# A gated hybrid encoder block on one core: the output product by seven products of quarters, and the first head's group four groups later

## Chip, core and metric

One Trainium2 chip, of which the kernel uses one core. The metric is the time of one execution in microseconds (us). A core has a matrix engine (TensorE, PE in the profile, PEld for its weight loads), a vector engine (VectorE, DVE), a scalar engine (ScalarE, ACT), GpSimd (POOL) and SyncE (SP), which here only issues transfers. Each engine works through its own row of instructions in order and waits at semaphores for the others; DMA engines move data between DRAM and the on-chip memory.

## What is computed

For 512 tokens of width 2048, all in float32:

```python
n = rmsnorm(x, norm_w)
proj = n @ w_in                       # gated DeltaNet, mLSTM and gate columns
y_a = gdn_branch(...)                 # 8 heads, conv of width 5, delta rule in chunks of 64, both directions
y_b = mlstm_branch(...)               # 8 heads, both directions
gates = sigmoid(gates + gate_bias)
merged = gates[0] * (y_a @ w_branch_gdn) + gates[1] * (y_b @ w_branch_mlstm)
x = x + merged @ w_out                # merged 512 x 2048, w_out 2048 x 2048
return rmsnorm(x, final_norm_w)
```

The change is in `merged @ w_out` and in where one head of `gdn_branch` is placed.

## The kernel before

Every large product is done with operands split in two: a high part, rounded to TensorE's fast float32 format, and a low part, the rest. A product of two split operands is three matmuls, high x high, high x low and low x high. Weights come in blocks of 512 KB (128 x 1024 numbers). `Block.load` (L160) brings a block into one of four raw buffers (`wr`), four blocks ahead (`LOAD_AHEAD`). `Block.split`, two blocks ahead (`SPLIT_AHEAD`), casts it to `wh` on ScalarE (L175) and subtracts to `wl` on VectorE (L176); three buffers each. Then the block's matmuls read both, first all of `wh`, then all of `wl`. A list `blocks` holds the blocks in the order of use: input projection, gates, branch products, output product.

Beside this stream run the heads, written as a generator (`master`). `tick()` lets it go on by one step after every fourth matmul of the projections (`TICK`), so the program order mixes head work and projection matmuls; a scheduler of the framework then sets each engine's row by its own priorities. `gdn_pre(h)` (the group at L485 to L498: products `pgm`, transposes `px`, `pq` of one GDN head) waits four ticks after `gv` of its head is done. `conv` (L427) makes `cv` by four tap operations on VectorE (L431) and an activation on ScalarE (L445). `ml_head(h)` (L802) does one mLSTM head: it loads `e` from `d_row`, makes `kw` (L853), states `msp` (L867) copied to `cn` (L872), and the outputs `ph`.

`br_evac` (L1007) multiplies the branch products by the gates and, for the second branch, splits their sum `merged` into `mh` and `ml`.

The output product has four column blocks e of 512, each with eight weight blocks of two k-tiles. Per block and row tile t of four there are six matmuls (`o_mms`, L1054), four row tiles accumulate in four PSUM banks, and after the eighth block `residual` (L1060) adds the product to x on VectorE, squares it on ScalarE and multiplies by the norm's weights. For e = 3 the eight blocks are kept, so that each row tile runs its 48 matmuls in one go and is then finished (`finish`: L1068 to L1076) while the next one runs. The tail of the kernel is the finish of row tile 3.

## Time and profile before

| | us |
|---|---|
| median of 3 runs | 1692.74 (1691.44 to 1692.97) |
| the profiled execution | 1691.47 |
| its span, first to last instruction | 1689.7 |
| TensorE busy | 1663.9 |
| VectorE busy | 863.7 |
| ScalarE busy | 627.2 |
| first matmul of the output product, from the span's start | 1506.07 |
| DMA traffic | 251.93 MB, mean 149 GB/s |

The span is what lies between the first and the last instruction; the execution's own time is 1.8 us longer. TensorE is the engine that is nearly always busy, the others are far from it on the mean, but they need not be in every stage. Matmuls overlap, so the duration of one (0.39 us) is longer than the step from one to the next. "Granted clock" is the share of full speed that TensorE's clock was given.

### The profile page before, as it was taken

How to read it: one execution, taken by the hardware profiler on the slowest of the kernel's cores; microseconds unless marked ns; L12 is line 12 of the kernel's file. 1: busy time of each engine (PE TensorE's matmuls, PEld its weight loads, DVE VectorE, ACT ScalarE, POOL GpSimd, SP SyncE). 2: the span in 40 equal slices, each digit the busy share in tenths (PEclk: the TensorE clock that was granted, in tenths of full speed). 3: DMA queues.
4: the chain of work that ended last, by engine and by line, in shares of the span. 5: the costliest groups of instructions: out<-in, count | busy, mean ns of one | idle time of the engine just before them, and what ended most of it. 6: DMA issues, size and time to landing. Idle time of an engine off the chain costs nothing.

```text
span 1689.7 us, 20934 instructions
## 1 busy us (share of the span) xinstructions
PE 1663.9 (98%) x8218; PEld 1397.3 (83%) x8218; DVE 863.7 (51%) x1259; ACT 627.2 (37%) x973; POOL 84.0 (5%) x117
## 2 busy tenths in 40 slices
PE   6999999999999999999999999999999999999998
PEld 6878888888888888888888888888888888888886
DVE  6866555669993344322444544544544444443342
ACT  6654444423333223334343344334234322222231
POOL 1110111000100000001000000000000000000000
PEclk9999999999999999999999999999999999999999
DMA  7576767594548767335343334434335544453322
GB/s 191 148 203 190 206 173 193 141 302 139 137 131 214 211 217 225 102 92 177 96 114 107 107 102 116 118 92 116 87 101 160 184 149 147 139 193 144 100 100 100
DMA packets 334204, 251.93 MB, mean 149 GB/s; under 512 B 38968, under 2 KB 294329, under 8 KB 333081
## 3 DMA queue, kind: packets, MB, share of 16 engines
q1 hardware_dynamic: 327952, 238.39, 49.4%
q10 hardware_dynamic: 6153, 12.19, 2.2%
q8 instruction: 65, 1.06, 0.3%
q14 instruction: 34, 0.28, 0.1%
HBM read 207.32 MB, written 43.16 MB: 148 GB/s over the span
## 4 chain that ended last, share of the span: by engine, by line
PE 94%; DMA 2%; issue 1%; DVE 1%; ACT 1%; SPq 0%; ACTq 0%; POOL 0%; POOLq 0%; DVEq 0%
PE pj_m L212 26%; PE pj_mg L212 19%; PE pj_br L212 10%; PE wo L1054 9%; PE pj_gq L212 5%; PE pj_gz L212 5%; PE pj_gv L212 5%; PE pj_gk L212 4%; PE og L685 1%; PE vps L708 1%; PE ph L887 1%; DMA wr<-in_w_in_dram 1%; PE pgm L491 1%; PE pj_gk L1175 1%; PE ph L886 1%
## 5 line engine op out<-in xcount | busy, mean ns | idle before, releaser
L176 DVE TENSOR_TENSOR wl<-wr,wh 128x1024 fp32r<-128x1024 f32 x270 | 331.3, 1228 | 461.9 <-ACT wh L175 175.9
L175 ACT CAST wh<-wr 128x1024 fp32r<-128x1024 f32 x270 | 284.1, 1053 | 682.7 <-PE pj_m L212 207.5
L212 PE MATMUL pj_m<-nth,wh 128*128 128x512 f32 x640 | 250.5, 391 | 0.0
L212 PE MATMUL pj_m<-ntl,wh 128*128 128x512 f32 x640 | 249.1, 389 | 0.0
L212 PE MATMUL pj_mg<-nth,wh 128*128 128x512 f32 x512 | 204.0, 399 | 0.0
L212 PE MATMUL pj_mg<-ntl,wh 128*128 128x512 f32 x512 | 199.8, 390 | 0.0
L212 PE MATMUL pj_m<-nth,wl 128*128 128x512 f32 x640 | 160.2, 390 | 0.0
L212 PEld LDWEIGHTS pj_m<-nth,wh 128*128 128x128 f32 x640 | 120.2, 188 | 24.5
L212 PEld LDWEIGHTS pj_m<-ntl,wh 128*128 128x128 f32 x640 | 120.2, 188 | 24.4
L212 PEld LDWEIGHTS pj_m<-nth,wl 128*128 128x128 f32 x640 | 119.6, 188 | 24.6
L212 PE MATMUL pj_mg<-nth,wl 128*128 128x512 f32 x512 | 126.7, 389 | 0.0
L212 PEld LDWEIGHTS pj_mg<-nth,wl 128*128 128x128 f32 x512 | 96.1, 188 | 20.3
L212 PEld LDWEIGHTS pj_mg<-nth,wh 128*128 128x128 f32 x512 | 96.3, 188 | 18.9
L212 PEld LDWEIGHTS pj_mg<-ntl,wh 128*128 128x128 f32 x512 | 96.3, 188 | 18.4
L1054 PE MATMUL wo<-wh,mh 128*128 128x512 f32 x256 | 100.0, 391 | 0.0
L1054 PE MATMUL wo<-wh,ml 128*128 128x512 f32 x256 | 99.6, 389 | 0.0
L212 PE MATMUL pj_br<-yh,wh 128*128 128x512 f32 x256 | 99.6, 389 | 0.0
L212 PE MATMUL pj_br<-yl,wh 128*128 128x512 f32 x256 | 99.6, 389 | 0.0
L1054 PE MATMUL wo<-wl,mh 128*128 128x512 f32 x256 | 72.9, 390 | 0.2 <-DVE wl L176 0.2
L1019 DVE TENSOR_TENSOR mgr<-pj_br,mgr 128x512 f32<-128x512 f32 x32 | 22.1, 692 | 86.5 <-PE pj_br L212 86.5
L212 PE MATMUL pj_br<-yh,wl 128*128 128x512 f32 x256 | 63.2, 389 | 0.0
L1054 PEld LDWEIGHTS wo<-wl,mh 128*128 128x128 f32 x256 | 48.0, 188 | 10.9 <-DVE wl L176 0.6
(321 smaller groups left out, 2513.6 us busy)
## 6 DMA issues: line engine op xcount, KB each, us to landing
wr<-in_w_in_dram SPq DMA_DIRECT2D x206, 512.0 KB, 4.1
wr<-in_w_out_dram SPq DMA_DIRECT2D x32, 512.0 KB, 3.7
hr<-d_head SPq DMA_DIRECT2D x16, 768.0 KB, 5.8
d_gate<-gt ACTq DMA_DIRECT2D x32, 256.0 KB, 2.2
e<-d_row SPq DMA_DIRECT2D x8, 1024.0 KB, 5.5
mgr<-d_gate SPq DMA_DIRECT2D x32, 256.0 KB, 4.8
wr<-in_w_branch_gdn_dram SPq DMA_DIRECT2D x16, 512.0 KB, 4.4
wr<-in_w_branch_mlstm_dram SPq DMA_DIRECT2D x16, 512.0 KB, 4.5
```

The lines of the kernel that those rows point to most:

```text
L175: nc.scalar.copy(hi[:, 0:m], self.raw[:, 0:m])
L176: nc.vector.tensor_tensor(lo[:, 0:m], self.raw[:, 0:m], hi[:, 0:m].bitcast(F32), op=ALU.subtract)
L212: nc.tensor.matmul(ps[0:m, :], l, r, start=(first and n == 0), stop=(last and n == len(jobs) - 1))
L491: nc.tensor.matmul(pgm[t // 2][:, t % 2], ckq[:, 0, cs], ckq[:, :, cs], start=True, stop=True)
L685: nc.tensor.matmul(po[:, t], l, r, start=not opened, stop=last)
L708: nc.tensor.matmul(vps[:, d], xt[:, d, t], rhs[d], start=True, stop=True)
L886: nc.tensor.matmul(ph[:, j - q0, :], e4[:, d, 1, t, :], cn[d][1][:, n - 1, :], start=True, stop=False)
L887: nc.tensor.matmul(ph[:, j - q0, :], e4[:, d, 0, t, :], vv[:, t, :], start=(n == 0), stop=True)
L1019: nc.vector.tensor_tensor(g_, ps, g_, op=ALU.mult)
L1054: nc.tensor.matmul(ps, l[:, kt, ts_], r, start=(kt == 0 and l is mh and r is hv), stop=(kt == NK - 1 and r is lv))
L1175: nc.tensor.matmul(pk[:, ts_], w, act[:, kt, ts_], start=not opened, stop=last)
```

## The change

**The output product.** `merged` (512 x 2048) and `w_out` (2048 x 2048) are cut into quarters: token halves (256 rows) by even and odd 128-wide k-tiles on one side, even and odd k-tiles by column halves within each half e of 1024 columns on the other. By the scheme of Strassen in Winograd's form the 2 x 2 product of quarters is made with seven products in place of eight; four of the seven use sums of quarters of `w_out`, four use sums of quarters of `merged`. Each of the two halves e is done so, in the order of products `OUT_ORDER`. A product is four weight blocks of two row tiles p, 12 matmuls per block. The number of weight blocks goes from 32 to 56.

**Sums of w_out.** They depend on nothing but the input, and are made in sixteen parts within `ml_head`, two per head: `quarter_load` (three transfers on SyncE, 1 MB in all), `quarter_sums` (three VectorE operations), `quarter_store` (one transfer of 1 MB on SyncE into a DRAM buffer `d_t`). The blocks of the last stage are then loaded from `w_out` or `d_t`.

**Sums of merged.** `br_evac` keeps `merged` in float32 (`mf`), casts what the first products need and adds the quarters in place; `s_split` splits the four sums during the first eight blocks of the last stage. x and the final norm's weights come in during the first half, in parts.

**Evacuation.** Products are added to x as they come (`out_evac`, `add_to`), products 1, 6 and 7 by way of a running sum `u`. Row tiles 0 and 1 are done with product 3 of the second half; the last product keeps its four blocks and runs row tile by row tile, so that only tiles 2 and 3 are finished at the end.

**The first head's group.** `gdn_pre(0)` waits for eight ticks, not four.

```diff
@@ gdn_pre
-        for _ in range(4):
+        for _ in range(8 if h == 0 else 4):
             yield
@@ ahead of ml_head
+    def quarter_load(q):
+        e, j = q // 8, q % 8
+        qt = st["p3"][1].tile([P, 4, 512], F32, tag="qt", name=f"qt{q}", bufs=2)
+        c = e * 1024
+        nc.sync.dma_start(qt[:, 0:2].rearrange("p a c -> p (a c)"), wo4[j, 0][:, c:c + 1024])
+        nc.sync.dma_start(qt[:, 2], wo4[j, 1][:, c + 512:c + 1024])
+        nc.sync.dma_start(qt[:, 3], wo4[j, 1][:, c:c + 512])
+    def quarter_sums(q):
+        ts = st["p3"][1].tile([P, 4, 512], F32, tag="qs", name=f"qs{q}", bufs=2)
+        nc.vector.tensor_tensor(ts[:, 0:2], qt[:, 1:3], qt[:, 0:2], op=ALU.subtract)
+        nc.vector.tensor_tensor(ts[:, 2], qt[:, 2], ts[:, 0], op=ALU.subtract)
+        nc.vector.tensor_tensor(ts[:, 3], ts[:, 2], qt[:, 3], op=ALU.subtract)
+    def quarter_store(q):
+        nc.sync.dma_start(d_t[q // 8, :, q % 8].rearrange("i p c -> p i c"), st.pop(("qs", q)))
@@ ml_head
+        quarter_load(2 * h)
         while f"m0{h}" not in done:
             yield
         e = p3.tile([P, 2, 2, T], F32, tag="e", name=f"e{h}", bufs=2)
...
+        quarter_load(2 * h + 1)
         for _ in range(6):
             yield
+        quarter_sums(2 * h)
...
+        quarter_store(2 * h)
         while f"m1{h}" not in done:
             yield
+        quarter_sums(2 * h + 1)
...
+        quarter_store(2 * h + 1)
@@ br_evac, second branch
+                nc.vector.tensor_tensor(mf[:, n], st["g", 0], g_, op=ALU.add)
+                (hi, lo), src = (st["a2"], mf[:, n]) if n % 2 else (st["a1"], mf[:, n, 0:256])
+                nc.scalar.copy(hi[:, j], src)
+                nc.vector.tensor_tensor(lo[:, j], src, hi[:, j].bitcast(F32), op=ALU.subtract)
+                if n % 2:
+                    nc.vector.tensor_tensor(a22, a21, a22, op=ALU.add)
+                    nc.vector.tensor_tensor(a21, a11, a21, op=ALU.subtract)
+                    nc.vector.tensor_tensor(a11, a22, a11, op=ALU.subtract)
+                    nc.vector.tensor_tensor(a12, a12, a11, op=ALU.subtract)
@@ output product
+    OUT_ORDER = ((1, 4, 2, 5, 6, 3, 7), (1, 5, 2, 6, 3, 7, 4))
+    def s_split(n):
+        nc.scalar.copy(hi[:, js], src)
+        nc.vector.tensor_tensor(lo[:, js], src, hi[:, js].bitcast(F32), op=ALU.subtract)
+    def out_mms(i, p, jobs, first, last):
+        for n, (j, v, lo) in enumerate(jobs):
+            for a in (ah,) if lo else (ah, al):
+                nc.tensor.matmul(st["po", i, p], a[:, j, ts_], v, ...)
+            if (e, i) == (1, 4):
+                st["last"] = st.get("last", []) + his + los
+                if b < 3:
+                    return
+                for p in range(2):
+                    out_mms(i, p, st["last"], True, True)
+                    out_evac(e, i, p)
+                return
+            for jobs in (his, los):
+                for p in range(2):
+                    out_mms(i, p, jobs, b == 0 and jobs is his, b == 3 and jobs is los)
+    for e in range(2):
+        for pos in range(7):
+            for b in range(4):
+                blocks.append(Block(... out_src(e, OUT_ORDER[e][pos], b) ..., 2, 512, out_use(e, pos, b), ...))
@@ finish
-        nc.scalar.activation(rt[:, 0:768], rt[:, 0:768], AF.Identity, scale=fr)
-        nc.scalar.dma_start(rows[:, 0:768], rt[:, 0:768])
+        nc.scalar.activation(rt[0][t], rt[0][t], AF.Identity, scale=fr)
+        nc.scalar.dma_start(rows[:, 0:1024], rt[0][t])
```

How the rows of the engines move, at three places. The numbers behind the names count tiles and differ between the two kernels.

TensorE at the first GDN head's group, before: the transposes of `cv` (`px`) stand behind 16 matmuls on `wh` and one on `wl` of the unit `gk`, after that the unit `gq` begins.

```order
L212 MATMUL pj_gk_861<-ntl,wh_819 128x512
L212 MATMUL pj_gk_861<-nth,wl_820 128x512
L495 MATMUL px_889<-ident,cv_847 128x128 [waits Activation_49]
L495 MATMUL px_889<-ident,cv_847 128x128 x3
L212 MATMUL pj_gk_861<-nth,wl_820 128x512 x7
L212 MATMUL pj_gq_991<-nth,wh_857 128x512 [waits DVE_49]
L212 MATMUL pj_gq_991<-ntl,wh_857 128x512
L212 MATMUL pj_gq_991<-nth,wh_857 128x512
```

The same place after:

```order
L500 MATMUL px_911<-ident,ckq_691 128x128 x4
L503 MATMUL pq_921<-ident,ckq_691 128x128 x4
L217 MATMUL pj_gk_862<-nth,wh_820 128x512
L217 MATMUL pj_gk_862<-ntl,wh_820 128x512
L500 MATMUL px_912<-ident,cv_848 128x128 [waits Activation_49]
L500 MATMUL px_912<-ident,cv_848 128x128 x3
L217 MATMUL pj_gk_862<-nth,wh_820 128x512
L217 MATMUL pj_gk_862<-ntl,wh_820 128x512
L217 MATMUL pj_gk_862<-nth,wl_821 128x512 x8
L217 MATMUL pj_gq_976<-nth,wh_858 128x512 [waits DVE_49]
L217 MATMUL pj_gq_976<-ntl,wh_858 128x512
```

The group stands later in the unit: ten matmuls of `gk` are left behind `px`, where there were seven.

VectorE in the same group, before, between the taps of `cv` (L431) and the `la` products, and then after, where L436 and L510 are those lines:

```order
L431 SCALAR_TENSOR_TENSOR ca_g_848<-pj_gv_789,cwg,ca_g_848 128x510 [waits Activation_49]
L505 TENSOR_TENSOR la_903<-pgm_882,dec_589 128x512 [waits PE_49,Pool_49]
L431 SCALAR_TENSOR_TENSOR ca_g_848<-pj_gv_789,cwg,ca_g_848 128x511 [waits DVE_49]
L505 TENSOR_TENSOR la_903<-pgm_882,dec_589 128x512 [waits Pool_49]
L431 SCALAR_TENSOR_TENSOR ca_g_848<-pj_gv_789,cwg,ca_g_848 128x511 [waits DVE_49]
L505 TENSOR_TENSOR la_903<-pgm_883,dec_589 128x512 [waits PE_49]
L431 SCALAR_TENSOR_TENSOR ca_g_848<-pj_gv_789,cwg,ca_g_848 128x510 [waits DVE_49]
L505 TENSOR_TENSOR la_903<-pgm_883,dec_589 128x512
L176 TENSOR_TENSOR wl_918<-wr_817,wh_917 128x1024 [waits PE_49,Activation_49]
```

```order
L436 SCALAR_TENSOR_TENSOR ca_g_849<-pj_gv_790,cwg,ca_g_849 128x510 [waits Activation_49]
L181 TENSOR_TENSOR wl_890<-wr_818,wh_889 128x1024 [waits PE_49,Activation_49]
L436 SCALAR_TENSOR_TENSOR ca_g_849<-pj_gv_790,cwg,ca_g_849 128x511 [waits DVE_49] x2
L436 SCALAR_TENSOR_TENSOR ca_g_849<-pj_gv_790,cwg,ca_g_849 128x510 [waits DVE_49]
L510 TENSOR_TENSOR la_926<-pgm_905,dec_590 128x512 [waits PE_49,Pool_49]
L510 TENSOR_TENSOR la_926<-pgm_905,dec_590 128x512 [waits Pool_49]
L510 TENSOR_TENSOR la_926<-pgm_906,dec_590 128x512 [waits PE_49]
L510 TENSOR_TENSOR la_926<-pgm_906,dec_590 128x512
```

The `la` operations have left the places between the taps, and a `wl` has come there.

VectorE in the first mLSTM head, before, from a `wl` by `kw` (L853) and `e` to the copies `cn`:

```order
L176 TENSOR_TENSOR wl_6629<-wr_6561,wh_6628 128x1024 [waits DMAHW1_49,PE_49,Activation_49]
L853 TENSOR_TENSOR kw_6659<-mkt_6656,ksc 128x512 [waits Activation_49]
L853 TENSOR_TENSOR kw_6659<-mkt_6656,ksc 128x512
L857 SCALAR_TENSOR_TENSOR e_6487<-psc_6643,e_6487 128x512 [waits PE_49,Pool_49]
L857 SCALAR_TENSOR_TENSOR e_6487<-psc_6643,e_6487 128x512 [waits Pool_49]
L872 COPY cn_6677<-msp_6676 128x129 [waits PE_49]
L874 SCALAR_TENSOR_TENSOR cn_6677<-cn_6677,mud,msp_6676 128x129 [waits DVE_49]
L872 COPY cn_6682<-msp_6681 128x129 [waits PE_49]
L874 SCALAR_TENSOR_TENSOR cn_6677<-cn_6677,mud,msp_6676 128x129 [waits DVE_49]
L874 SCALAR_TENSOR_TENSOR cn_6682<-cn_6682,mud,msp_6681 128x129 [waits DVE_49]
```

After (`qs` and `qt` are the sums and loads of a quarter, L823 to L825 `quarter_sums`):

```order
L181 TENSOR_TENSOR wl_6647<-wr_6574,wh_6646 128x1024 [waits DMAHW2_49,PE_49,Activation_49]
L823 TENSOR_TENSOR qs_7890<-qt_7729 128x1024 [waits DMAHW6_49,DMAHW3_49,DMAHW1_49]
L888 TENSOR_TENSOR kw_6678<-mkt_6675,ksc 128x512 [waits Activation_49]
L888 TENSOR_TENSOR kw_6678<-mkt_6675,ksc 128x512
L892 SCALAR_TENSOR_TENSOR e_6492<-psc_6662,e_6492 128x512 [waits PE_49,Pool_49]
L892 SCALAR_TENSOR_TENSOR e_6492<-psc_6662,e_6492 128x512 [waits Pool_49]
L824 TENSOR_TENSOR qs_7890<-qt_7729,qs_7890 128x512 [waits DVE_49]
L825 TENSOR_TENSOR qs_7890<-qs_7890,qt_7729 128x512 [waits DMAHW7_49,DVE_49]
L907 COPY cn_6696<-msp_6695 128x129 [waits PE_49]
L823 TENSOR_TENSOR qs_7948<-qt_7856 128x1024 [waits DMAHW4_49,DMAHW2_49,DMAHW1_49]
L907 COPY cn_6701<-msp_6700 128x129 [waits PE_49]
L909 SCALAR_TENSOR_TENSOR cn_6696<-cn_6696,mud,msp_6695 128x129 [waits DVE_49]
```

A quarter's sums, which wait for transfers (DMAHW), stand ahead of `kw` and amid the copies `cn`.

SyncE at the same head, before, from the load of `e` on:

```order
L807 DMA e_6487<-d_row 128x2x1024 [waits DMAHW3_49,PE_49]
L166 DMA wr_6279<-in_w_in_dram 128x8x128 [waits DMAHW5_49,DMAHW4_49,DVE_49]
L807 DMA e_6918<-d_row 128x2x1024 [waits DMAHW6_49,PE_49,Pool_49]
L166 DMA wr_6310<-in_w_in_dram 128x8x128 [waits DMAHW7_49,DVE_49]
L166 DMA wr_6343<-in_w_in_dram 128x8x128 [waits DMAHW0_49,DVE_49]
L166 DMA wr_6374<-in_w_in_dram 128x8x128 [waits DMAHW2_49,DVE_49]
L166 DMA wr_6407<-in_w_in_dram 128x8x128 [waits DMAHW5_49,DMAHW3_49,DVE_49]
L166 DMA wr_6438<-in_w_in_dram 128x8x128 [waits DMAHW7_49,DVE_49]
```

After (L815 to L817 `quarter_load`, L829 `quarter_store`):

```order
L815 DMA qt_6213<-in_w_out_dram 128x1024 [waits DMAHW2_49,DMAHW3_49,DMAHW1_49,PE_49]
L816 DMA qt_6213<-in_w_out_dram 128x512 [waits DMAHW5_49]
L817 DMA qt_6213<-in_w_out_dram 128x512 [waits DMAHW6_49]
L171 DMA wr_6284<-in_w_in_dram 128x8x128 [waits DMAHW7_49,DMAHW4_49,DVE_49]
L837 DMA e_6492<-d_row 128x2x1024 [waits DMAHW0_49,PE_49]
L171 DMA wr_6315<-in_w_in_dram 128x8x128 [waits DVE_49]
L815 DMA qt_6494<-in_w_out_dram 128x1024
L816 DMA qt_6494<-in_w_out_dram 128x512 [waits DMAHW3_49]
L817 DMA qt_6494<-in_w_out_dram 128x512 [waits DMAHW4_49]
L171 DMA wr_6348<-in_w_in_dram 128x8x128 [waits DMAHW5_49,DVE_49]
L829 DMA d_t<-qs_6528 128x4x512 [waits DMAHW6_49]
L829 DMA d_t<-qs_6586 128x4x512 [waits DMAHW0_49,DVE_49]
```

Loads and stores of quarters stand between the weight loads. All sixteen quarters lie so between row 355 and row 449 of this engine, with 26 weight loads.

VectorE at the end of the program, before, from the last `wl` to the finish of the first row tile and the sum of the second:

```order
L176 TENSOR_TENSOR wl_12191<-wr_12178,wh_12190 128x1024 [waits DMAHW6_49]
L176 TENSOR_TENSOR wl_12195<-wr_12184,wh_12194 128x1024 [waits DMAHW7_49]
L1088 TENSOR_REDUCE fpart<-fss 128x4
L1089 TENSOR_SCALAR fpart<-fpart 128x4 [waits DVE_49]
L1060 TENSOR_TENSOR rt_11394<-rt_11394,wo_12202 128x512 [waits PE_49]
L1068 TENSOR_SCALAR fr_12253<-fss,fpart 128x1 [waits Activation_49]
L1072 SCALAR_TENSOR_TENSOR rt_11394<-rt_11394,fr_12253,fw 128x512 [waits Pool_49]
L1076 TENSOR_SCALAR rt_11394<-rt_11394,fr_12253 128x768
L1060 TENSOR_TENSOR rt_11395<-rt_11395,wo_12262 128x512 [waits PE_49]
```

After, from within the evacuation of product 7 to the sum of row tile 2 (L1202, L1139, L1134 are `out_evac`, `add_to`, `weigh`):

```order
L1139 TENSOR_TENSOR rt_11777<-rt_11777,u_12259 128x512
L1139 TENSOR_TENSOR rt_11778<-rt_11778,u_12261 128x512 [waits DVE_49]
L1134 TENSOR_TENSOR rt_11777<-rt_11777,fw 128x512 [waits Activation_49]
L1173 TENSOR_TENSOR fq_12688<-fq_12688,fss 128x1
L1139 TENSOR_TENSOR rt_11778<-rt_11778,u_12261 128x512
L1174 TENSOR_SCALAR fq_12688<-fq_12688 128x1 [waits DVE_49]
L1134 TENSOR_TENSOR rt_11778<-rt_11778,fw 128x512 [waits Activation_49]
L1173 TENSOR_TENSOR fq_12697<-fq_12697,fss 128x1
L181 TENSOR_TENSOR wl_12702<-wr_12647,wh_12701 128x1024 [waits DMAHW2_49]
L1174 TENSOR_SCALAR fq_12697<-fq_12697 128x1 [waits DVE_49]
L181 TENSOR_TENSOR wl_12708<-wr_12665,wh_12707 128x1024 [waits DMAHW3_49]
L1139 TENSOR_TENSOR rt_11777<-rt_11777,po_12705 128x512 [waits PE_49]
```

The last two `wl` stand behind the evacuation of the product before.

TensorE at the end, before, where row tile 2 ends and row tile 3 begins (48 matmuls each):

```order
L1054 MATMUL wo_12322<-wh_12194,ml 128x512
L1054 MATMUL wo_12322<-wl_12195,mh 128x512
L1054 MATMUL wo_12322<-wh_12194,mh 128x512
L1054 MATMUL wo_12322<-wh_12194,ml 128x512
L1054 MATMUL wo_12322<-wl_12195,mh 128x512
L1054 MATMUL wo_12382<-wh_12096,mh 128x512
L1054 MATMUL wo_12382<-wh_12096,ml 128x512
```

After, where the last product (`po_12705` row tile 2, `po_12706` row tile 3) needs its last two `wl`; row 5484 is its first matmul, row 5527 its last:

```order
L1213 MATMUL po_12706<-wh_12667,a_10399 128x512
L1213 MATMUL po_12706<-wl_12668,a_10398 128x512
L1213 MATMUL po_12705<-wl_12702,a_10398 128x512 [waits DVE_49]
L1213 MATMUL po_12705<-wl_12702,a_10398 128x512
L1213 MATMUL po_12705<-wh_12707,a_10398 128x512 [waits Activation_49]
L1213 MATMUL po_12705<-wh_12707,a_10399 128x512
L1213 MATMUL po_12705<-wh_12707,a_10398 128x512
L1213 MATMUL po_12705<-wh_12707,a_10399 128x512
L1213 MATMUL po_12705<-wl_12708,a_10398 128x512 [waits DVE_49]
L1213 MATMUL po_12705<-wl_12708,a_10398 128x512
L1213 MATMUL po_12706<-wl_12668,a_10398 128x512
L1213 MATMUL po_12706<-wh_12701,a_10398 128x512
```

Row tile 3 is run in part ahead of the last matmuls of row tile 2, and 13 matmuls are left behind them.

## Rows read from the trace of the kernel before

**Rows 1.** Page, busy time: engine, busy us (share of the span), instructions:

```profile
PE 1663.9 (98%) x8218; PEld 1397.3 (83%) x8218; DVE 863.7 (51%) x1259; ACT 627.2 (37%) x973; POOL 84.0 (5%) x117
```

**Rows 2.** Chain of waits, last stage: start us, us, what, count:

```profile
1506.23 123.50 PE wo L1054 x544
1640.58 29.88 PE wo L1054 x129
1672.80 10.43 issue
```

**Rows 3.** Windows of L1054: stretch, us, PE, PEld busy, granted clock, DMA share, GB/s:

```profile
1506.00:1681.50 175.50, 175.18 (x768) 143.84 (x768) 1.00 0.35 126
```

**Rows 4.** TensorE's waits: what waits <- for what: us, times, longest:

```profile
PE px L495 <- ACT cv L445: 3.0, 1, 3.0
```

**Rows 5.** Chain of waits, GDN stage:

```profile
137.65 10.88 PE pj_gv L212 x48
```

**Rows 6.** Timeline of TensorE, first output matmul: start us, us, what:

```profile
1506.07 0.39 PE L1054 MATMUL wo<-wh,mh 128*128 128x512 f32 x1
```

**Rows 7.** Timeline of VectorE, end of the program: ... [idle before <-releaser]:

```profile
1635.64 2.48 DVE L1060 TENSOR_TENSOR rt<-rt,wo 128x512 f32<-128x512 f32 x4
...
1670.48 0.69 DVE L1060 TENSOR_TENSOR rt<-rt,wo 128x512 f32<-128x512 f32 x1 [7.36 <-PE wo L1054]
...
1681.50 0.69 DVE L1060 TENSOR_TENSOR rt<-rt,wo 128x512 f32<-128x512 f32 x1 [7.38 <-PE wo L1054]
...
1684.52 0.61 DVE L1076 TENSOR_SCALAR rt<-rt,fr 128x768 f32<-128x768 f32 x1
```

**Rows 8.** Timeline of ScalarE, last finish:

```profile
1683.85 0.94 ACT L1074 ACTIVATE rt<-rt,fr 128x768 f32<-128x768 f32 x1 [0.91 <-POOL fr L1069]
```

**Rows 9.** Page, costliest groups: instruction xcount | busy us, mean ns | idle before:

```profile
L176 DVE TENSOR_TENSOR wl<-wr,wh 128x1024 fp32r<-128x1024 f32 x270 | 331.3, 1228 | 461.9 <-ACT wh L175 175.9
L175 ACT CAST wh<-wr 128x1024 fp32r<-128x1024 f32 x270 | 284.1, 1053 | 682.7 <-PE pj_m L212 207.5
```

**Rows 10.** Windows, SyncE: stretch, us, granted clock, DMA share, GB/s:

```profile
1514.00:1518.00 4.00, 1.00 1.00 418
1518.00:1522.00 4.00, 1.00 1.01 426
...
510.00:520.00 10.00, 1.00 1.00 204
763.00:775.00 12.00, 1.00 0.94 320
...
763.00:920.00 157.00, 1.00 0.46 128
```

**Rows 11.** Page, DMA queue of ScalarE: packets, MB, share of 16 engines' span:

```profile
q10 hardware_dynamic: 6153, 12.19, 2.2%
```

**Rows 12.** Timeline of VectorE, first mLSTM head:

```profile
804.94 1.23 DVE L176 TENSOR_TENSOR wl<-wr,wh 128x1024 fp32r<-128x1024 f32 x1 [4.22 <-PE pj_m L212]
...
834.96 1.29 DVE L853 TENSOR_TENSOR kw<-mkt,ksc 128x512 f32<-128x512 f32 x2 [1.60 <-ACT mkt L848]
```

**Rows 13.** Timeline of TensorE, first mLSTM head:

```profile
819.19 1.98 PE L212 MATMUL pj_m<-nth,wl 128*128 128x512 f32 x8
...
838.21 1.50 PE L867 MATMUL msp<-va,kw 128*128 128x129 f32 x12
```

**Rows 14.** Timeline of TensorE, first GDN head's group:

```profile
88.77 0.66 PE L495 MATMUL px<-ident,cv 128*128 128x128 f32 x4 [3.05 <-ACT cv L445]
...
90.88 0.39 PE L212 MATMUL pj_gq<-nth,wh 128*128 128x512 f32 x1
```

**Rows 15.** Timeline of ScalarE, same place:

```profile
86.79 1.28 ACT L445 ACT_TABLE_LOAD   x1
```

**Rows 16.** Timeline of VectorE, same place:

```profile
82.06 0.73 DVE L431 SCALAR_TENSOR_TENSOR ca_g<-pj_gv,cwg,ca_g 128x510 f32<-128x510 f32 x1
...
85.82 0.73 DVE L431 SCALAR_TENSOR_TENSOR ca_g<-pj_gv,cwg,ca_g 128x510 f32<-128x510 f32 x1
```

More of the change, by code (lines that the diff above doesn't have):

```diff
@@ L95, in hybrid_block @@
     d_y = dram.tile([2, H, P, T], F32, name="d_y")
+    d_t = dram.tile([2, 4, 8, P, 512], F32, name="d_t")
     st = {}
@@ L1065, in finish, with open_final2 @@
-    def finish(t):
-        rt, fss, fw = st["rt"][t], st["fss"], st["fw"]
-        fr = st["fp"][1].tile([P, 1], F32, tag="fr", name=f"fr{t}", bufs=4)
-        nc.vector.tensor_scalar(fr, fss[:, t, 3:4], 1.0 / DM, st["fpart"][:, t:t + 1], op0=ALU.mult, op1=ALU.add)
+    def open_final2():
+        close_pool("mfp")
+        rp = open_pool("rp", side="left")
+        st["rt"].append([rp.tile([P, 1024], F32, name=f"rt1{t}") for t in range(NT)])
+        st["fw"] = rp.tile([P, DM], F32, name="fw")
@@ new lines, in weigh, with add_to @@
+    def weigh(t, e):
+        nc.vector.tensor_tensor(piece(t, e), piece(t, e), st["fw"][:, e * 512:e * 512 + 512], op=ALU.mult)
+    def add_to(t, e, v, op=ALU.add):
+        r = piece(t, e)
+        nc.vector.tensor_tensor(r, r, v, op=op)
+        parts_in[t, e] = parts_in.get((t, e), 0) + 1
+        if parts_in[t, e] < (3 if t < 2 and e % 2 else 2):
+            return
+        nc.scalar.activation(st["fsq"], r, AF.Square, accum_out=st["fss"][:, t, e:e + 1])
+        if e < 2:
+            later.append(lambda: weigh(t, e))
+        elif e == last_e(t):
+            finish(t)
+        else:
+            weigh(t, e)
@@ L1108, in hybrid_block @@
-    for e in range(4):
-        for k2 in range(8):
-            blocks.append(Block([wo2[k2 * 256:(k2 + 1) * 256, e * 512:(e + 1) * 512]], 2, 512, o_use(e, k2),
-                                open_final if (e, k2) == (0, 0) else None, 5 if e == 3 and k2 >= 3 else None))
+        lp, op_ = piece(t, le), piece(t, 5 - le)
+        nc.vector.scalar_tensor_tensor(lp, lp, fr, fw[:, le * 512:le * 512 + 512], op0=ALU.mult, op1=ALU.mult)
+        nc.sync.dma_start(rows[:, le * 512:le * 512 + 512], lp)
@@ L1270, in hybrid_block @@
     close_pool("fp")
+    close_pool("sp")
+    close_pool("rp")
     close_pool("mp")
```

188 lines of the change are left out of this document (127 added, 61 removed).

## Prediction

> **What bounds the kernel now.** First the page's busy shares: TensorE is busy for 98% of the span [rows 1], so nothing shortens the kernel that doesn't take TensorE work away, shorten one of its few waits, or shorten the tail behind its last matmul. Then the chain of waits, to see whether the stage that is changed lies on it: the output product is two pieces of it, 544 and 129 matmuls, and it ends with 10.43 us in which TensorE has nothing left to do [rows 2]. The windows say how dense that stage is: 175.18 of 175.50 us busy, at a granted clock of 1.00 (the 2.4 GHz level), with the DMA engines at 0.35 [rows 3]. So it costs its number of matmuls. Last the list of TensorE's waits, because the change also moves the first gated-delta head: that head holds the one wait of 3.0 us in the steady part, for `cv` [rows 4].
>
> Price of a matmul: the chain has 48 in 10.88 us [rows 5], 226.7 ns each. In the output product 544 took 123.50, 227.0 each, and the last 129 took 29.88, 231.6 each [rows 2]: there the time ends with column block 3, where each matmul group ends in a finish of its own.
>
> **1. Fewer matmuls.** Before: 4 column blocks x 16 k-tiles x 4 row tiles x 3 = 768. After: 2 halves x 7 products x 4 weight blocks x 12 = 672. 96 x 0.2267 = 21.8 us come off the path, as all of it is on it. I count the whole last stage, from its first matmul at 1506.07 [rows 6] to the end of the span.
> Before: 1689.7 - 1506.07 = 183.6 us. Of it 768 x 0.2267 = 174.1 are matmuls, 1.3 small losses up to the last residual sum at 1681.50, and 8.2 the tail [rows 7].
> After: 672 x 0.2267 = 152.3, the same 1.3, and three things of its own.
> (a) A wait before the last product's second half: on VectorE the `wl` of its last two blocks stand behind the evacuation of product 7 (VectorE's order at the end of the program, shown with the change). That is eight operations of 128x512, at the pitch of four in 2.48 us [rows 7] 5.0 us, with three small ones about 5.5, and it can begin 0.4 us before the product's end, when its first half is done. The first `wl` (1.23 us [rows 9]) is then ready some 6.3 us after the product's end, the second at 7.5. TensorE's order has 27 matmuls ahead of the first, 6.1 us, and six more, 7.5 us, ahead of the second. So 0.3 to 1.5 us; I take 0.8.
> (b) Between the finishes of the last two row tiles lie 13 matmuls, 2.9 us, where there were 48, 11.02 us (1670.48 to 1681.50 [rows 7]). A finish holds VectorE from 1681.50 to 1685.13, 3.6 us [rows 7], so the last one starts about 0.55 us late.
> (c) ScalarE scales 1024 columns in the finish where it scaled 768 in 0.94 us [rows 8]: +0.3, and its transfer of 512 KB in place of 384: +0.1.
> After: 152.3 + 1.3 + 0.8 + 0.55 + 8.2 + 0.4 = 163.6. Gain 20.0 us. Bounds: 17 (0.231 per matmul, 96 x 0.231 = 22.2, less 5 for all of (a) to (c) doubled and another 1.5) to 22.5 (no a, no b, no loss).
>
> What could stop it inside the stage is named once: each block is now 12 matmuls, 2.72 us, and needs a cast of 1.05 on ScalarE, a subtraction of 1.23 on VectorE [rows 9] and 512 KB. In the first eight blocks the splitting of the four activation sums comes on top, as much again: 2.1 us on ScalarE and 2.46 on VectorE per 2.72. At a product's end at most six operations, 3.7 us, stand ahead of the next `wl` (products 4 and 2 of the first half are evacuated in other places by VectorE's order); with that `wl` 4.9 us, while TensorE has 24 + 8 matmuls, 7.25 us, until it reads it. 512 KB per 2.72 us are 193 GB/s, with x and the final norm's weights up to 340; 418 were seen there [rows 10]. So hidden, at a cost of nothing; the rival below prices it if not.
>
> **2. The sums of w_out, under the mLSTM heads.** 16 quarters, each 3 loads (1.05 MB), three VectorE operations (1.23 + 2 x 0.62 = 2.5 us) and one store of 1.05 MB. Their VectorE time is 40 us, and TensorE does not read them until the last stage. What hides them is the projection stream; uncovered they would cost all 40. By the order they don't spread over eight heads: all loads and stores stand between the first head's `e` and the third head's last weights, with 26 weight blocks, which before is 763 to 920 us.
> Bandwidth there: before 128 GB/s x 157 us = 20.1 MB [rows 10]; added 16 x 2.1 = 33.6 MB; together 53.7 MB, 342 GB/s. What the trace shows of rates: 418 in 1514 to 1518 (loads alone), 320 at a share of 0.94, so 340 when full, in 763 to 775 (mixed) [rows 10]; ScalarE's queue, which holds only stores, 12.19 MB in 2.2% of the span [rows 11], 328. So 128 us at the highest and 158 at the mixed rate: the DMA engines are nearly full for the whole stretch, but a late weight is not yet a wait: the `wl` made at 804.94 to 806.17 [rows 12] is read at 819.19 [rows 13], 13.0 us later.
> The Trainium skill, in "DMA: Bandwidth & Descriptors", section Bandwidth, says that for transfers between HBM and SBUF the HBM side binds, at about 358 GB/s per core. The 418 and 426 of this trace [rows 10] exceed that; by 358 the stretch would take 150 us of its 157 and term 2 would stay what it is.
> VectorE's row: a sum waits for its load, and behind it in the row stand `wl`, `kw` and the small copies of the head. In head 0 the first sum of a quarter stands right ahead of `kw`: `kw` ends at 836.25 [rows 12] and TensorE's `msp` reads it at 838.21 [rows 13], 2.0 us of slack, of which the sum itself takes 1.2. If its load is late by more than 0.8 us, TensorE waits. On SyncE's row the stores wait for the sums and the next weight load stands behind them; four raw buffers at 5.44 us cover that.
> Cost: nothing at best, 12 at worst (stretch at 340 with the row's waits added, about three heads x 4 us). I take 1.5, nearer to the free end, because the slack of 13 us is larger than the 1 us by which 158 exceeds 157.
>
> **3. The first head's group, four groups later.** The 16 matmuls between fill time, but they are only moved. What ends the wait for `cv` is a chain on other engines: VectorE's four tap operations (first 82.06, last 85.82), ScalarE's table load 86.79 of 1.28 us, `cv` itself, then `px` at 88.77 [rows 14 to 16]. In the new order three operations on `la` (3 x 0.6 us) between the taps are gone and one `wl` (1.13) stands there in their place, so `px` comes 0.65 us earlier, at 88.1. But TensorE then has 10 matmuls of that unit left, not 7: `gq` starts at 88.1 + 0.4 + 10 x 0.2267 = 90.8, against 90.88 [rows 14]. Gain 0.1 (bounds: a loss of 0.5, a gain of 1.3). `la` comes later, which the solve behind it reads; the wait list shows no wait of TensorE for it.
>
> **4. The merge of the branches.** Per pair of rows four VectorE operations of 128x256 more, at most 4 x 0.62 = 2.5 us, beside 96 matmuls, 21.8 us. Hidden.
>
> **Sum.** 1691.47 (the profiled execution: span 1689.7 and 1.8 around it) - 20.0 + 1.5 - 0.1 = 1672.9. The median of the runs shown is 1.27 above the profiled one: **1674**. Own range 1670 to 1677.5.
>
> **Rivals.**
> *A. The burst of transfers reaches TensorE.* The stretch 763 to 920 is near full, and VectorE's row is in order, so one late load of a quarter holds `wl` and `kw` too. For it: 342 GB/s asked where 340 were seen, and a slack of 0.8 us at `kw`. Against: 13 us of slack for weights. In three heads 2 to 5 us each, 6 to 15: 1679 to 1689.
> The Trainium skill ("TensorE: Matmul & The Clock Gate", table at its head) gives VectorE a strictly first-in-first-out queue, eight deep, which is the mechanism that A needs; no row of this trace shows an operation overtaking another there.
> *B. Stores are far slower than loads* (slower than before). In 510 to 520 the engines were full at 204 GB/s [rows 10], beside the GDN solve; the windows don't say what slowed them. If the d_t stores run so, 16.8 MB take 82 us and the other 36.9 MB at 340 108: 191 us for 157, and 34 - 13 = 21 us late, as much as the product saves; with the in-order row of A's 6 more, 1700. It decides from about 205 GB/s down. Against: ScalarE's queue, which holds stores alone, shows 328.
> *C. The moved group does save the wait.* If `cv` is already there when TensorE reaches `px`, up to 3.0 us [rows 4]: 1671.
> *D. VectorE or ScalarE bounds the last stage.* 90% of VectorE is asked for in the first eight blocks, and a late `wl` costs TensorE at each heavy product's end. 2 to 3 us at three or four of them, 4 to 12: 1678 to 1686.
>
> **How the numbers follow.** Forecast 0.55 (1670 to 1677.5), A 0.22, D 0.10, C 0.06, B 0.07. A measurement of this kernel tells about 0.2% from no change, 3.4 us; faster then means below 1689.3. A quarter of A, 0.05, ends there or above it, B is slower: faster 0.88, same 0.05, slower 0.07. Range for 8 in 10: from 1668 (the gain's bound of 22.5 with C's part) to 1687 (A and D but for A's last quarter); outside are B and some 0.06 of A and C.
>
> **What would show it.** Output product: 672 matmuls in about 154 us; first matmul to end of span about 163.6. In the list of waits no `wl` over 2 us in that stage. In 763 to 920: DMA share 0.9 or more, and TensorE's waits for `wl`, `wh` or `kw` together under 3 us; 6 or more is A, and a GB/s near 200 in it is B. `px` still waiting near 3 us right behind the moved group (C would leave none), and `gq` within 0.5 us of 90.9. Waits at the ends of products 7 and 5 are D. The prediction is wrong if the matmuls of the last stage are not 227 ns apart, or the sums cost more than 5 us.

## The result

| | us |
|---|---|
| kernel before, beside it | 1692.3 median of 4 (1691.44 to 1692.97) |
| changed kernel | 1672.84 median of 4 (1671.73 to 1674.2) |
| ratio | 0.9886, 95% interval 0.9869 to 0.9903 |
| profiled execution, its span | 1674.2, 1672.5 |

The kernel is 1.1% faster, and the interval lies below 1. The forecast was 1674, with 1670 to 1677.5 for the likeliest case. Two later rounds of the same kernel gave 1671.58 and 1672.03. So the whole came out nearly as worked out; the terms did not, quite. The chain of waits of the changed kernel, from 751.99 us on (start us, us, what, count; shorter pieces are left out), beside [rows 2]:

```profile
763.77 25.42 PE pj_mg L217 x112
792.75 7.04 DMA qt<-in_w_out_dram
803.71 5.55 DMA wr<-in_w_in_dram
817.91 4.95 DMA qt<-in_w_out_dram
833.21 6.08 DMA qt<-in_w_out_dram
...
897.25 6.30 DMA qt<-in_w_out_dram
912.66 48.09 PE pj_m L217 x212
...
1511.25 149.63 PE po L1213 x659
```

New in it are the loads of quarters (`qt`) between 793 and 903 us: there the chain leaves TensorE. In the chain of the kernel before, the two projection pieces that begin here at 763.77 and 912.66 are these:

```profile
761.31 38.10 PE pj_mg L212 x168
...
907.64 48.09 PE pj_m L212 x212
```

So between these two marks, which bound the stretch of the sums, 912.66 - 763.77 - (907.64 - 761.31) = 2.56 us were lost, and 2.46 up to the first mark. The last stage begins 5.0 us later than before.

The last stage, in windows of the lines that make it (stretch, us, PE and PEld busy, granted clock, DMA share, GB/s), beside [rows 3]:

```profile
1511.10:1663.80 152.70, 152.70 (x672) 125.82 (x671) 1.00 0.68 221
```

672 matmuls in 152.70 us, 227.2 ns each, and TensorE busy all of it. From its first matmul to the end of the span: 1672.5 - 1511.1 = 161.4 us, where it was 183.6. That is 22.2 us less; with the 5.0 us lost earlier the span is 17.2 us shorter (1689.7 to 1672.5). The profiled execution was the slowest of the four.

TensorE's list of waits (what waits <- for what: us in total, times, longest), beside [rows 4]:

```profile
PE px L500 <- ACT cv L450: 3.6, 1, 3.6
PE msp L902 <- DVE kw L888: 2.1, 2, 1.5
```

No `wl` of the last stage is in it. The wait of `msp` for `kw` is new; it is the one that rival A named.

### The profile page after: what moved, and what is told of

Read it like the earlier page. It is cut to its first block, busy times and chain, and to the rows that moved or that the text cites. A ratio compares the mean times of both kernels' runs of the same rounds, so it can differ in the third digit from the quotient of the medians.

```text
span 1672.5 us, 21141 instructions
## 1 busy us (share of the span) xinstructions
PE 1643.9 (98%) x8122; PEld 1380.9 (83%) x8122; DVE 965.0 (58%) x1409; ACT 663.5 (40%) x1012; POOL 87.2 (5%) x117
## 4 chain that ended last, share of the span: by engine, by line
PE 89%; DMA 5%; DVE 3%; issue 1%; SPq 1%; ACT 1%; POOL 0%; POOLq 0%; DVEq 0%; ACTq 0%
PE pj_m L217 21%; PE pj_mg L217 19%; PE pj_br L217 10%; PE po L1213 9%; PE pj_gq L217 5%; PE pj_gz L217 5%; PE pj_gv L217 5%; PE pj_gk L217 4%; DMA qt<-in_w_out_dram 2%; PE og L690 1%; PE vps L713 1%; PE ph L922 1%; DVE wl L181 1%; PE pgm L496 1%; PE pj_gk L1334 1%
## 5 line engine op out<-in xcount | busy, mean ns | idle before, releaser
L181 DVE TENSOR_TENSOR wl<-wr,wh 128x1024 fp32r<-128x1024 f32 x294 | 360.1, 1227 | 353.8 <-ACT wh L180 191.9
L180 ACT CAST wh<-wr 128x1024 fp32r<-128x1024 f32 x294 | 309.2, 1053 | 634.2 <-PE pj_m L217 182.2
L1054 DVE TENSOR_TENSOR mgr<-pj_br,mgr 128x512 f32<-128x512 f32 x32 | 22.1, 690 | 78.1 <-PE pj_br L217 78.1
L1213 PE MATMUL po<-wh,s 128*128 128x512 f32 x256 | 63.2, 389 | 0.0
L217 PEld LDWEIGHTS pj_br<-yl,wh 128*128 128x128 f32 x256 | 48.1, 188 | 10.0
L1213 PEld LDWEIGHTS po<-wh,s 128*128 128x128 f32 x256 | 48.1, 188 | 10.0
L217 PEld LDWEIGHTS pj_br<-yh,wl 128*128 128x128 f32 x256 | 48.0, 188 | 10.0
```

Source lines behind the costliest of these rows:

```text
L180: nc.scalar.copy(hi[:, 0:m], self.raw[:, 0:m])
L181: nc.vector.tensor_tensor(lo[:, 0:m], self.raw[:, 0:m], hi[:, 0:m].bitcast(F32), op=ALU.subtract)
L217: nc.tensor.matmul(ps[0:m, :], l, r, start=(first and n == 0), stop=(last and n == len(jobs) - 1))
L1054: nc.vector.tensor_tensor(g_, ps, g_, op=ALU.mult)
L1213: nc.tensor.matmul(st["po", i, p], a[:, j, ts_], v, start=(first and n == 0 and a is ah), stop=(last and n == len(jobs) - 1))
```

## What was tried

Three questions were left: what the sums under the heads really cost and why; what the moved group does, since TensorE reached `gq` at 92.51 us and not at 90.8; and how much of either is the execution and not the kernel. All kernels ran against the kernel before on their own chip.

| kernel | median us | ratio to before (95%) | lost in the stretch of the sums | wait of `px` | granted clock 88 to 94 |
|---|---|---|---|---|---|
| changed | 1672.84 | 0.9886 (0.9869 to 0.9903) | 2.56 | 3.6 | 0.73 |
| changed, second time | 1671.58 | 0.9874 (0.9861 to 0.9888) | 2.05 | 3.8 | 0.72 |
| changed, third time | 1672.03 | 0.9878 (0.9863 to 0.9893) | 1.68 | 3.6 | 0.72 |
| group4 | 1671.52 | 0.9868 (0.9853 to 0.9883) | 0.36 | 3.5 | 0.50 |
| group16 | 1670.71 | 0.986 (0.9845 to 0.9875) | 0.87 | 1.7 at another head | 1.00 |
| no_sums | 1671.15 | 0.9862 (0.9847 to 0.9877) | 0.0 | 3.6 | 0.50 |
| spread | 1670.43 | 0.9858 (0.9841 to 0.9874) | 0.0 | 3.7 | 0.74 |
| spread16 | 1669.11 | 0.9863 (0.9849 to 0.9876) | 0.0 | 1.8 at another head | 0.73 |
| store_twice | 1671.31 (2 runs) | 0.9874 (0.9856 to 0.9892) | 0.0 | 3.5 | 0.72 |
| before_sums | 1694.22 | 1.0008 (0.9999 to 1.0017) | 2.72 | 3.8 | 0.72 |
| row2 | 1668.51 | 0.9858 (0.9843 to 0.9873) | 0.0 | 1.8 | 1.00 |
| spread_row2 | 1669.09 | 0.986 (0.9844 to 0.9877) | 0.0 | 2.3 | 0.90 |

The last three columns are from the one profiled execution of each kernel, the loss by the two marks above. The times of single executions of one kernel lie 1 to 4 us apart, so the intervals overlap, and what is told apart below is told from the traces; the times only bear the size of it.

### The stretch of the sums

**no_sums**: no quarter is loaded, added or stored, and the last stage reads slices of `w_out` in place of the sums, so its output is not the product.

```diff
-        quarter_load(2 * h)
...
-        return d_t[e, {5: 0, 7: 1, 6: 2, 4: 3}[i], js].rearrange("j p c -> p j c")
+        c = e * 1024 + (512 if i in (5, 6) else 0)
+        return wo2.rearrange("(j a p) c -> a p j c", a=2, p=P)[i % 2][:, js, c:c + 512]
```

> The changed kernel without the sums of w_out: no loads, sums or stores of quarters under the mLSTM heads, and the last stage loads slices of w_out where it loaded d_t (the output is not the product then). Theory: the sums cost what TensorE lost in 763 to 912 us, 2.56 us, most of it two waits of msp for kw (2.1): this kernel 2.5 us faster than the changed one, about 1670.3, no msp wait. Rival: the DMA traffic costs nothing and the 2.56 us come from the earlier parts: within 0.5 us of the changed kernel. Second rival, the sums also lengthen other stages (buffers, scheduling): 4 us or more.

The stretch took 146.33 us, to 0.01 what it took before, and no `msp` is in the list of waits. So all that is lost between the marks is due to the sums.

**before_sums**: the kernel before, with the quarters made in its heads and read by nothing (the functions and calls of the diff ahead of `ml_head` and in it, and `d_t`).

> The kernel before with the quarter loads, sums and stores added in its mLSTM heads, and nothing that reads them. Theory: they cost what TensorE loses between the first and the third mLSTM head, 0.4 to 2.6 us against the kernel before, DMA share 0.95 or more there, waits of msp for kw or none. Rival: without the later product and group order the cost is nothing within 0.3 us, or above 5 us.

2.72 us were lost between the marks, with `msp` waiting 2.2 us for `kw`. The time is 0.08% above the kernel before (1694.22 against 1692.63, interval 0.9999 to 1.0017), which by itself is not told apart from nothing. By the trace the sums cost the same without the rest of the change.

**spread**: the two loads of a head tied behind the load of that head's `e` in SyncE's row.

```diff
-        quarter_load(2 * h)
...
-        nc.sync.dma_start(e, d_row[:, h].partition_broadcast(P))
+        el = nc.sync.dma_start(e, d_row[:, h].partition_broadcast(P))
+        with tc.issue_after(el.ins if hasattr(el, "ins") else el):
+            quarter_load(2 * h)
+            quarter_load(2 * h + 1)
...
-        quarter_load(2 * h + 1)
```

> The changed kernel with each head's two quarter loads tied behind the load of that head's e on SyncE, so that two quarters go with each of eight heads (about 5 MB per 61 us) and not sixteen with the first two and a half heads. Theory: what TensorE loses is VectorE standing at a quarter whose load is late because the DMA engines are full (share 0.97 to 1.05 in 783 to 903); with 4.2 MB added per head the share falls to 0.6 or so and the waits of msp for kw go: 2 us faster than the changed kernel. Rival: it is the place of the sum ahead of kw in VectorE's row, not the load on the DMA engines: the wait comes back in each head, 0.5 to 1.5 us each, so 2 to 8 us slower than the changed kernel.

Nothing was lost, and no wait for `kw` is left. The changed kernel's trace shows where the wait came from: VectorE ahead of `kw` in the first mLSTM head (start us, us, what, [idle before <- releaser]), beside [rows 12]:

```profile
839.42 1.23 DVE L823 TENSOR_TENSOR qs<-qt 128x1024 f32<-128x1024 f32 x1 [3.59 <-DMA qt<-in_w_out_dram]
840.56 1.29 DVE L888 TENSOR_TENSOR kw<-mkt,ksc 128x512 f32<-128x512 f32 x2
```

and then TensorE in it, beside [rows 13]:

```profile
841.39 1.58 PE L902 MATMUL msp<-va,kw 128*128 128x129 f32 x12 [0.56 <-DVE kw L888]
```

VectorE stood 3.59 us for a quarter's load with `kw` behind the sum in its row, and TensorE then 0.56 us for `kw`. In the second head a quarter's three sums, a `wl` and one more operation stand ahead of `kw`; there VectorE stood 4.47 us, and TensorE 1.52 us:

```profile
899.26 1.23 DVE L823 TENSOR_TENSOR qs<-qt 128x1024 f32<-128x1024 f32 x1 [4.47 <-DMA qt<-in_w_out_dram]
...
903.47 1.28 DVE L888 TENSOR_TENSOR kw<-mkt,ksc 128x512 f32<-128x512 f32 x2
```

VectorE's list of waits in 760 to 960 us says how common the first half of this is:

```profile
DVE qs L823 <- DMA qt<-in_w_out_dram: 34.9, 10, 4.7
```

Ten sums waited 34.9 us, and of that 2.1 reached TensorE as waits. In spread VectorE still waits, for less, and at places where nothing that TensorE wants stands behind it:

```profile
DVE qs L823 <- DMA qt<-in_w_out_dram: 10.2, 7, 3.5
```

So the edit did two things at once: it took load off the DMA engines (a share of 0.69 over 763 to 920 us, where it was 0.97), and it took the sums away from ahead of `kw`. Spread alone does not say which of the two removed the wait.

**store_twice**: each quarter's sums are stored a second time, into a buffer `d_u`.

```diff
+    d_u = dram.tile([2, 4, 8, P, 512], F32, name="d_u")
...
-        nc.sync.dma_start(d_t[q // 8, :, q % 8].rearrange("i p c -> p i c"), st.pop(("qs", q)))
+        nc.sync.dma_start(d_t[q // 8, :, q % 8].rearrange("i p c -> p i c"), st["qs", q])
+        nc.sync.dma_start(d_u[q // 8, :, q % 8].rearrange("i p c -> p i c"), st.pop(("qs", q)))
```

> The changed kernel with each quarter's sums stored twice, the second time into a buffer that nothing reads: 16.8 MB more in the stretch of the sums. Theory: the DMA engines are full there (0.97 of 763 to 920 us), so 16.8 MB at 330 GB/s add 51 us of transfers, and behind the slack of some 13 us TensorE waits for weights, about 30 to 40 us slower than the changed kernel, waits for wl or wh in the list. Rival: the stretch only grows longer and the weights keep their lead, since the quarters give way: under 10 us slower, with the wait still at kw alone.

The theory fell. No time was lost at all, though the DMA engines were nearly as full, and for longer. The windows (stretch, us, granted clock, DMA share, GB/s), the changed kernel:

```profile
823.00:843.00 20.00, 1.00 1.01 332
...
903.00:923.00 20.00, 1.00 1.00 332
923.00:943.00 20.00, 1.00 0.81 245
943.00:963.00 20.00, 1.00 0.39 99
```

and with the stores doubled:

```profile
823.00:843.00 20.00, 1.00 0.96 316
...
903.00:923.00 20.00, 1.00 0.93 309
923.00:943.00 20.00, 1.00 1.01 332
943.00:963.00 20.00, 1.00 0.92 298
963.00:983.00 20.00, 1.00 1.02 349
```

With more to store the stretch is longer: fewer quarters stand between the same weight loads (35 issues of quarter loads in 763 to 925 us, 48 in the changed kernel), the rest come later. So full DMA engines alone cost nothing here; the weights keep their lead. Nor does the place of a sum ahead of `kw` cost by itself: in store_twice's first head VectorE stood 2.49 us for a load right ahead of `kw`, and TensorE did not wait. What costs is a sum whose load is late by more than the slack, at one of the places where `kw` stands behind it.

How late the loads are differs from trace to trace. group4, group16 and row2 have the same order of VectorE and SyncE in this stretch as the changed kernel, and lost 0.36, 0.87 and 0.0 us; the changed kernel lost 2.56, 2.05 and 1.68 in three executions. The loss goes with what VectorE waited for `qt` in all (L823, 760 to 960 us): 34.9, 33.7 and 33.9 us in these three, 35.5 in before_sums, against 32.0 in group16, 29.2 in group4 and 26.5 in row2. What makes the loads later in one trace than in another, with the same order, stays open.

### The first head's group

**group4**: `for _ in range(4)` for all heads, as before the change.

> The changed kernel with the first head's group back at four ticks, nothing else. Its trace has TensorE wait 3.57 us for cv behind the moved group (3.05 before), the granted clock at 0.66 in 88.3 to 92.6 (1.00 before), and gq starts at 92.51 against 90.88. Theory 1, the move costs 1.6 us, because the later group makes the idle time longer and the clock falls behind it: this kernel is 1.6 us faster than the changed one (about 1671.2), px waits 3.0 to 3.1, clock 1.00 behind it, gq at 90.9. Theory 2, the 1.6 us are a difference from one execution to the next or come from other parts of the change: the same time as the changed kernel, and a low clock behind px here too. Theory 3, as predicted, the move gains 0.1: slower by 0.1, not to be told apart from 2 by the time but by the clock.

Theory 2 holds. `px` waits 3.5 us here too, the clock behind it is lower still, and `gq` begins at 92.56 us, as late as in the changed kernel. Windows of TensorE (stretch, us, PE busy, granted clock, DMA share, GB/s), the kernel before, the changed one and group4:

```profile
88.00:94.00 6.00, 5.23 (x25) 1.00 0.75 182
```

```profile
88.00:94.00 6.00, 5.60 (x21) 0.73 0.53 105
```

```profile
88.00:94.00 6.00, 5.34 (x15) 0.50 0.78 191
```

In 6 us of a busy TensorE 25 matmul records stand at the full clock, 21 and 15 at the lower ones. After the wait of 3.05 us in the profiled execution of the kernel before [rows 14] the clock stayed at 2.4 GHz; after the waits of 3.5 to 3.8 us in the others it was at 1.2 GHz for part or all of the 6 us. before_sums has, up to 95 us, the instructions of the kernel before in the same order on every engine; still it waited 3.8 us, had 0.72, and began `gq` at 91.91 us, where before took 90.88. So the 1.6 us by which `gq` came late are not the move's: group4 has them without it, and the larger part arises between two executions of the same order. Of the kernel before there is one trace only; the changed kernel showed the low clock in all three.

The Trainium skill, "TensorE: Matmul & The Clock Gate", section "Part 1: The HAM clock gate", says that the array falls back to the slower clock after idling and regains it by activity; the windows agree that it falls behind idling and comes back with the matmuls (0.66 in 88.3 to 92.6 us of the changed kernel, 1.00 in 92.6 to 98). The length of the wait alone doesn't decide here: the clock fell behind waits of 2.0 (spread16), 2.3 (spread_row2) and 3.5 to 3.8 us, and stayed at 1.00 behind 1.8 (group16, row2) and 3.05 (the profiled execution of before).

**group16**: sixteen ticks in place of eight.

> The changed kernel with the first head's group sixteen ticks later in place of eight. cv is there at 88.35 us in the trace of the changed kernel; sixteen ticks bring the group some 7 us further, to about 88.5 or later, behind four matmuls on wl of the unit gq. Theory: TensorE's wait for cv of 3.6 us and the low clock behind it (1.4 us) both go: 5.0 us faster than the changed kernel, about 1667.9, no px in the list of waits. Rival: the wait goes elsewhere, since the same chain on VectorE (tap operations, wl) holds the next unit's first matmul or its wl: gain under 2 us and a new wait of 2 to 3 us in 84 to 95 us.

The rival holds, with two waits under 2 us in place of one of 2 to 3. `cv` is there when the group comes, but the next unit's first matmul waits for the same tap operations, 1.8 us, since they free its PSUM bank, and the next head's `px` waits 1.7 us. The clock stayed at 1.00. The waits of group16:

```profile
PE pj_gq L217 <- DVE ca_g L436: 1.8, 1, 1.8
...
PE px L500 <- ACT cv L450: 1.7, 1, 1.7
```

**row2**: the cause is further up. In the changed kernel's trace, VectorE and then ScalarE (start us, us, what, [idle before <- releaser]):

```profile
74.94 1.57 DVE L390 TENSOR_TENSOR_SCAN row<-rst,lf_r 8x512 f32<-8x512 f32 x1
...
78.64 0.54 DVE L404 TENSOR_TENSOR row<-row,mu 8x384 f32<-8x384 f32 x1
```

```profile
79.21 0.63 ACT L406 ACTIVATE row<-row 8x512 f32<-8x512 f32 x1 [1.18 <-DVE row L404]
79.75 0.66 ACT L434 ACTIVATE ca_g<-pj_gv,cwg 128x512 f32<-128x512 f32 x1
```

The second direction's scan in the mLSTM setup (L390) writes into the only `row` buffer, which is free when the first direction's store `d_row` has landed. The chain of the kernel before shows that step (start us, us, what; the scan is L385 there):

```profile
69.06 6.22 DMA d_row<-row
...
75.37 1.34 DVE row L385
```

In the changed kernel's trace the scan follows a `wl` on VectorE; that it hangs on the store there too is shown by the edit below. On ScalarE `cv`'s first operation (L434) stands behind the activation of that chain.

```diff
-            row = su.tile([H, 2, T], F32, tag="row", name=f"row{d}")
+            row = su.tile([H, 2, T], F32, tag="row", name=f"row{d}", bufs=2)
```

> The changed kernel with two buffers in place of one for the mLSTM setup's row tile, which the group's wait for cv seems to hang on: the second direction's scan waits for the store of the first (d_row, 6.2 us), ScalarE's activation on row waits for that chain, and cv's first operation stands behind it in ScalarE's row. Theory: with a buffer of its own the chain starts some 4 us earlier, cv is there near 84 to 85 us, the wait of px falls from 3.6 to under 1 us and the clock stays at 1.00 behind it: 3.5 to 5 us faster than the changed kernel. Rival: the chain is bound by VectorE's own work there (small operations of 1.2 us that take 0.2 elsewhere), so cv comes less than 1.5 us earlier and the time moves by under 1.5 us.

The scan begins at 65.29 us in place of 74.94. `px` waits half as long, the clock stays up, and `gq` starts at 88.56 us in place of 92.51:

```profile
85.08 0.66 PE L500 MATMUL px<-ident,cv 128*128 128x128 f32 x4 [1.76 <-ACT cv L450]
...
88.56 0.39 PE L217 MATMUL pj_gq<-nth,wh 128*128 128x512 f32 x1
```

1668.51 us against 1672.03 of the changed kernel on the same chip: 3.5 us, the theory's lower end. Not all of it need be the edit's: the profiled executions lie 5.5 us apart (spans of 1670.4 and 1664.9), 4.3 of them at `gq` (92.90 against 88.56) and 1.7 in the stretch of the sums, which the edit does not touch. The wait is 1.8 and not under 1: behind the taps `cv` still waits for an activation `dec` and the table load.

### Again, and together

> The changed kernel once more, on the same chip as the three below. Theory: what differs between executions is the clock behind the wait for cv (0.50 to 1.00 in 88 to 94 us over the traces so far) and the waits for kw (0.36 to 2.6 us lost in the stretch of the sums, in the changed kernel and in those with the group at four or sixteen ticks); so its median lies within 2 us of 1672.84, and of the two waits in its trace at least one differs by 0.5 us from the first trace. Rival: both are the same in every execution of one kernel: px wait 3.6, msp for kw 2.1, clock 0.73 in 88 to 94.

> The changed kernel a third time, as the measure for the two below on the same chip. Theory: 1671 to 1673, wait for cv 3.5 to 3.8 us, a granted clock under 1.00 somewhere in 86 to 96 us; loss in the stretch of the sums 0.4 to 2.6 us.

The clock was 0.72 in both, so that alone does not vary in this kernel as it was thought to; the losses in the stretch of the sums do, by 0.9 us over three executions.

**spread16** and **spread_row2** join spread with group16 and with row2.

> The changed kernel with both edits that helped: quarter loads tied to each head's e, and the first head's group at sixteen ticks. Theory: the two gains are in different places and add up: no wait of msp for kw, no wait over 2 us before 100 us, clock 1.00 in 88 to 94; 2.5 to 4 us faster than the changed kernel on the same chip. Rival: the group's gain is given back by the solve, which starts later with the later la: less than 1.5 us.

> Both edits together: quarter loads tied to each head's e, and two row buffers. Theory: they act in different places and add, 4.5 to 7 us faster than the changed kernel on the same chip, near 1666, no wait of TensorE above 1 us after the startup but for the solve's. Rival: the earlier row chain moves the wait to the next unit (as at sixteen ticks): under 3 us.

spread16 took 1669.11 against 1671.58 of the changed kernel on the same chip, 2.5 us less, the lower end. The clock fell to 0.73 all the same, behind a wait of `gq` of 2.0 us. spread_row2 took 1669.09, 2.9 less than the changed kernel and no less than row2 alone: the gains did not add. Row2's own trace had lost nothing in the stretch of the sums, so there was nothing to gain there; and in spread_row2 `px` waited 2.3 us, the clock fell (0.73 in 84 to 88 us, 0.79 in 88 to 91), and `gq` began at 90.92. That is 2.36 later than in row2, and the spans of the two profiled executions differ by 2.4 (1667.3 and 1664.9). So that the clock stays up with two row buffers held in one trace of two. The best of all, by 0.6 us that its scatter (1666.66 to 1670.75) does not bear out, is row2; spread_row2 has the narrowest scatter of it (1668.63 to 1669.19).

## Why the prediction was right, and where its steps were off

- **Term 1, the product.** Right in kind, too small in size: 20.0 us forecast, 22.2 measured, near the bound of 22.5. The matmuls' 227 ns held, and the last stage had no wait of TensorE at all. The 1.3 us of small losses that I carried over from before were 0.36 (152.70 - 672 x 0.2267): about 0.5 of them lay at the old stage's one wait for a `wl`, 0.2 us long, in column block 3; the others are not followed up. The wait (a), taken at 0.8, was 0. Its working was about half a microsecond too long: the evacuation with its small operations took 5.0 us (1652.47 to 1657.48) and not 5.5. So the `wl` was ready at 1658.70, just before the 27 matmuls ahead of its first reader end, at 1658.85:

```profile
1652.47 1.28 DVE L1202 TENSOR_TENSOR u<-u,po 128x512 f32<-128x512 f32 x2 [1.06 <-PE po L1213]
...
1657.48 1.22 DVE L181 TENSOR_TENSOR wl<-wr,wh 128x1024 fp32r<-128x1024 f32 x1
...
1664.39 0.68 DVE L1139 TENSOR_TENSOR rt<-rt,po 128x512 f32<-128x512 f32 x1
```

  The late start of the last finish (b) was there: the last matmul's group ends at 1663.81, the sum starts at 1664.39, 0.58 for the 0.55. (c) did not show: from that sum to the span's end 8.1 us, where before it was 8.2 [rows 7]; scaling 1024 columns took ScalarE 1.15 us in place of 0.94, and the transfer behind it was shorter by a little more.
- **Term 2, the sums.** The mechanism was right (the bandwidth near full, a late sum ahead of `kw`) and the size a little low: 1.5 taken, 2.56, 2.05 and 1.68 measured, 2.72 with the sums alone. The 0.8 us to spare were read too small: `msp` at 841.39 began ahead of the end of the second `kw` operation (840.56 + 1.29), so the first of the two is what it waits for, and about 0.6 us more were to spare. Rival A's wait came, but its price of 6 to 15 was wrong: only one or two of ten late sums had `kw` behind them. DMA share in 763 to 920 us was 0.97 as said; B did not come, with loads and stores together at 316 GB/s over the stretch:

```profile
763.00:920.00 157.00, 1.00 0.97 316
```

  That the DMA engines are nearly full, on which the worst case of this term was built, does not set its size: store_twice filled them longer at no cost, and row2 lost nothing at a share of 1.00.
- **Term 3, the group.** `px` came at 88.40, forecast 88.1. But `gq` came at 92.51, not 90.8: the step that failed is "10 x 0.2267" behind the wait. Those ten matmuls ran at a granted clock of 0.66 (windows: stretch, us, PE busy, granted clock, DMA share, GB/s, and the timeline):

```profile
88.30:92.60 4.30, 4.20 (x15) 0.66 0.50 91
```

```profile
88.40 1.11 PE L500 MATMUL px<-ident,cv 128*128 128x128 f32 x4 [3.57 <-ACT cv L450]
...
92.51 0.39 PE L217 MATMUL pj_gq<-nth,wh 128*128 128x512 f32 x1
```

  From `px` to `gq` it took 4.1 us where 2.7 were reckoned. The price of a matmul at full clock did hold at this place in the one trace of the kernel before [rows 14], behind a wait of 3.05 us; it held in none of the three traces of the changed kernel. So the prediction's own sign, `gq` within 0.5 us of 90.9, was missed. The error is not the move's: group4 has it too. Rival C did not come; `px` waited 3.6 us.
- **The rest.** 0.84 us more were lost in the GDN solve (417 to 540 us), where `pw` waits for a transfer: 1.5 us here, 0.9 in the kernel before, 0.2 to 1.1 in the traces of the experiments.
- **Rival D** was the narrowest miss the trace shows: VectorE was busy for 23.02 of the last stage's first 24 us, 96%, and TensorE still did not wait.

So the sum was right to 1.2 us partly because errors offset: term 1 was 2.2 us too low, and the losses ahead of the last stage, 1.4 in the sum, were 5.0 in the profiled execution. One step more was luck: the profiled execution was forecast at 1672.9 and took 1674.2, and the 1.27 us added to come to the median had the other sign here, where the median lies 1.36 below the profiled execution.

## What to carry to other kernels

Where one engine is busy all the time, count what is taken from it at the measured step, and look at each added operation not by how busy its engine is but by what stands behind it in that engine's row: here ten waits of 35 us in all cost 2 us, at the two places where the busy engine's next operand was queued behind. Full transfer engines did no harm to the weights, whose loads are issued four blocks ahead. A wait that a change does not remove is best followed to its first cause (here one buffer's reuse), since moving the waiting work moved the wait (group16). And a single trace is not the kernel: the clock behind the first wait differed between two executions of the same order, and the loss in the stretch of the sums between executions of one kernel.
